# Where the modulation of a group of k-tiles stands in VectorE's queue, in a float32 decoder layer on one core

## The chip, the cores and the metric

The kernel runs on one core of a Trainium2 chip. The metric is device time in microseconds, from one launch; 1799.18 us is the median of three runs of the kernel before (1798.88 to 1799.37).

## The reference, cut to what matters

One layer of a decoder trunk: 256 tokens, model width 2048, everything in float32. The part that the change touches is the first:

```
mod = silu(c) @ w_ada + b_ada            # (2048) @ (2048, 6*2048): shift, scale, gate, twice
h   = rmsnorm(x, g_mix) * (1 + sc1) + sh1
z   = h @ w_in                           # (256, 2048) @ (2048, 16392)
```

The columns of `z` feed three causal token mixers (an mLSTM, a differential attention, a stick-breaking attention) and three gates; their outputs are projected, summed under the gates, projected again and added to `x`. A gated MLP with a causal convolution follows, with shift, scale and gate of its own. The result is the residual stream, 256 by 2048.

## The kernel before, in words

Every large product is made of three passes over TensorE. A weight slab is cut into a high half, which ScalarE rounds (`A.copy`, L330), and a low half, the rest, which VectorE subtracts (L332). The activations are held as two halves too, `hi` and `lo` of `h`. High times high, low activations times high weights, and high activations times low weights are summed in PSUM. A slab has four k-tiles of 128 rows (or two, in the first visits) by 512 (or 440) columns; it is one transfer into a raw buffer (`weights`, L319 to L336), and the raw buffer comes free when the low half has been made. There are three raw buffers for slabs of four k-tiles, and the same three carry the modulation's weights; slabs of two k-tiles use another three. High and low halves have four buffers of two k-tiles each.

The modulation is a product of one row with a large matrix. It isn't made on TensorE: `ada_mac` multiplies each piece of `w_ada` by its column of silu(c) and adds it up on VectorE (L213 for the first piece of a group, L215 for the others). When the pieces of a group are done, TensorE sums over the partitions (`ada_sums`, L231), VectorE adds the biases and multiplies by g_mix (`b1` at L234, `a1` at L235 and L236), and `make_h` makes the group's `h` from the normalised and transposed x: ScalarE scales and shifts into a scratch tile (L439), rounds that to the high half, and VectorE subtracts to the low half (both in `split`, L393 and L394). The groups are k-tiles 0-1, 2-3, 4-7, 8-11 and 12-15.

Since h of later k-tiles is not there at the start, the first thirteen column blocks of `w_in` are made in visits: `visit` takes some blocks from the k-tile that they have reached to a later one, and `partial` adds what the visit brings to the sum kept in SBUF (L512, on VectorE), or leaves it in PSUM for the first two blocks (`kept`). The visits take blocks 0 to 8 to k-tile 2, blocks 9 to 12 to 4, blocks 0 to 8 to 4, blocks 0 to 9 to 8, blocks 10 to 12 to 12 and blocks 0 to 6 to 12; then every block is finished. So h of k-tiles 4-7 is first used by the slabs of blocks 0 and 1, 48 matmuls each. Between the slabs, `tick` draws pieces of the modulation out of a generator at a set rate, so that program order interleaves slabs, sums and pieces.

What runs when is settled when the kernel is built. A planner goes through the program with costs of its own and puts on each engine's queue what is ready by its reckoning, earlier instructions of the program first. On the chip each of VectorE's instructions then runs in that order, and waits for its inputs. `tc.issue_after(ins)` adds an edge for the planner alone: what is traced inside the block goes behind `ins` on the queue of that engine. The kernel before has such edges for the first visits (`hold`) and for the late modulation.

Of the kernel before, what the change touches and what calls it, by code (L numbers as in the profile page):

```python
# [13 lines left out]
ALU = mybir.AluOpType  # L14
# [4 lines left out]
S = 256  # L19
# [20 lines left out]
def kernel(  # L40
# [32 lines left out]
    def sidewide(name):  # L73
        return tmp.tile([P, 512], F32, tag="sidewide", name=name, bufs=4)

    def small(name):
        return tmp.tile([P, 256], F32, tag="small", name=name, bufs=3)

    V, A, T = nc.vector, nc.scalar, nc.tensor
# [44 lines left out]
    gmix_c = colsA[:, 0:16]  # L124
# [56 lines left out]

    side = deque()
    ada = deque()
    state = {"ada": 0.0, "side": 0.0, "split": None, "load": None, "hold": None, "h": 0, "started": False}

    def pump(queue, n):
        done = 0
# [12 lines left out]
    def tick():  # L200
        for key, queue in (("ada", ada), ("side", side)):
# [2 lines left out]
            state[key] -= n  # L204
            pump(queue, n)


    def ada_mac(accs, raw, kt0, nk):
        for k in range(nk):
            kt = kt0 + k  # L210
            acc = accs[kt % len(accs)]
            if kt < len(accs):
                V.tensor_scalar(acc, raw[:, k, :], ccol[:, kt:kt + 1], None, ALU.mult)  # L213
            else:
                state["mac"] = V.scalar_tensor_tensor(acc, raw[:, k, :], ccol[:, kt:kt + 1], acc, ALU.mult, ALU.add)  # L215

# [9 lines left out]
    def ada_sums(accs, k0, nk):  # L226

        pm = adaps.tile([P, 512], F32, tag="adaps", name="pm")
        for i, acc in enumerate(accs):
            for k in range(2 * nk):  # L230
                T.matmul(pm[:, k:k + 1], lhsT=acc[:, k * P:(k + 1) * P], rhs=ones[:, 0:1],  # L231
                         start=k + i == 0, stop=i == len(accs) - 1, skip_group_check=True)
        ks = slice(k0, k0 + nk)
        V.tensor_tensor(b1[:, ks], pm[:, 0:nk], bsh1_c[:, ks], ALU.add)  # L234
        V.tensor_tensor(a1[:, ks], pm[:, nk:2 * nk], bsc1_c[:, ks], ALU.add)  # L235
        V.tensor_tensor(a1[:, ks], a1[:, ks], gmix_c[:, ks], ALU.mult)  # L236
        make_h(k0, k0 + nk)

    def ada_first(k0):
# [78 lines left out]
    def weights(rows, nk, n, hold=None):  # L318
        if nk == 2:  # L319
            raw = adap.tile([P, 2, 512], F32, tag="ada", name="raw2")  # L320
        else:
            raw = rawp.tile([P, 4, 512], F32, tag="raw", name="raw")
        with tc.issue_after(state["load"].ins) if not state["started"] else nullcontext():
            state["started"] = True
            state["load"] = nc.sync.dma_start(raw[:, :nk, :n], rows.rearrange("(k p) f -> p k f", p=P))
        his, los = [], []
        for k0 in range(0, nk, 2):
            hi = hip.tile([P, 2, 512], F32R, tag="hi", name="hi")
            lo = lop.tile([P, 2, 512], F32R, tag="lo", name="lo")
            A.copy(hi[:, :, :n], raw[:, k0:k0 + 2, :n])  # L330
            with tc.issue_after(hold.ins) if hold else nullcontext():
                state["split"] = V.tensor_tensor(lo[:, :, :n], raw[:, k0:k0 + 2, :n], hi[:, :, :n].bitcast(F32),  # L332
                                                 ALU.subtract)
            his.append(hi)
            los.append(lo)
        return his, los  # L336
# [54 lines left out]
    def split(hi, lo, src):  # L391

        A.copy(hi, src)  # L393
        return V.tensor_tensor(lo, src, hi.bitcast(F32), ALU.subtract)  # L394
# [31 lines left out]
            A.copy(xnT[k2 // 4][:, (k2 % 4) * 512:(k2 % 4 + 1) * 512], pb)  # L426

    def make_h(kt0, kt1):
        ts = []
        for kt in range(kt0, kt1):  # L430
            t = small("ht")
            ts.append(t)
            hi, lo = hact[0](kt), hact[1](kt)
            if kt0 == 0:
                A.activation(hi, xnT_k(kt), AF.Identity, scale=a1[:, kt:kt + 1], bias=b1[:, kt:kt + 1])
                V.tensor_scalar(t, xnT_k(kt), a1[:, kt:kt + 1], b1[:, kt:kt + 1], ALU.mult, ALU.add)
                state["split"] = V.tensor_tensor(lo, t, hi.bitcast(F32), ALU.subtract)
            else:
                A.activation(t, xnT_k(kt), AF.Identity, scale=a1[:, kt:kt + 1], bias=b1[:, kt:kt + 1])  # L439
                state["split"] = split(hi, lo, t)  # L440
        if kt0 == 0:
            state["first"] = state["split"]
        state["h"] = kt1
# [44 lines left out]
    def shaped(src, dst):  # L488
        return src.rearrange("p (a b) -> p a b", a=dst.shape[1]) if len(dst.shape) == 3 else src

    def partial(ci, kt0, kt1):
# [12 lines left out]
        for b in range(2):  # L504
            for cs, d in dest(b):
                if ci in kept:
                    if kt1 == KD:
                        A.activation(d, shaped(acc[b][:, cs], d), AF.Copy, scale=scale)
                elif kt0 == 0:
                    A.activation(d, shaped(acc[b][:, cs], d), AF.Copy, scale=scale)  # L510
                else:
                    V.scalar_tensor_tensor(d, shaped(acc[b][:, cs], d), scale, d, ALU.mult, ALU.add)  # L512
        tick()

    kept = {}
# [325 lines left out]
            tick()  # L841


    rates["ada"] = 0.0
    def ada_rest():
        yield from ada_columns(3, bsh2_c, b2)
# [213 lines left out]
```

## Time and profile before

| what | value |
|---|---|
| median of three runs | 1799.18 us (1798.88 to 1799.37) |
| the profiled execution: its own time | 1798.04 us |
| the profiled execution: span from the first to the last instruction | 1796.1 us |
| TensorE matmuls busy | 1759.3 us, 98% of the span |
| VectorE busy | 1327.8 us, 74% |
| ScalarE busy | 909.8 us, 51% |
| mean granted TensorE clock | 0.993 |
| moved by DMA | 423.31 MB, 236 GB/s |

Busy time is the union of an engine's instructions; the rest of the span it stood idle. The profiled execution's own time is 1.9 us above its span. PE is TensorE, PEld its weight loads, DVE VectorE, ACT ScalarE, SPq the queue of SyncE, which issues the transfers of weights. L332 is line 332 of the kernel before. A row of a stretch has its start and end, its length, the busy time (and number of instructions) of PE, PEld, DVE, ACT and POOL, the granted clock as a share of 2.4 GHz, the share of time that the 16 DMA engines were busy, and GB/s. A row of the order in time has start and duration in us, engine, line, operation, names, shapes and, in brackets, how long the engine had been idle and what ended that.

### The profile page before, as it was taken

The numbers are of one execution on the slowest core, as the hardware profiler recorded it, in microseconds if no ns is written. First come the engines' busy times: TensorE is split into PE (matmuls) and PEld (weight loads), VectorE is DVE, ScalarE is ACT, GpSimd is POOL, SyncE is SP. The second block draws the span as 40 slices with busy tenths as digits, with TensorE's granted clock in tenths as the row PEclk, the third lists the DMA queues.
The fourth block names the chain that finished last, engine by engine and source line by source line (L and its number), as shares of the span: only waits on it lengthen the run. The fifth ranks groups of instructions, "written<-read, shape, count | busy, mean of one in ns | idle before, by whom it ended". The sixth has DMA issues, their size and how long they took to land.

```text
span 1796.1 us, 23640 instructions
## 1 busy us (share of the span) xinstructions
PE 1759.3 (98%) x9101; PEld 1506.9 (84%) x9101; DVE 1327.8 (74%) x1781; ACT 909.8 (51%) x1234; POOL 16.4 (1%) x44
## 2 busy tenths in 40 slices
PE   6989999999999999999999999999999999999998
PEld 5888999888878887888888878888888888888887
DVE  6899766888988788777896577888875556666654
ACT  6533345666565556544444455555553345555432
POOL 2000000000000000000000000000000000000000
PEclk8999999999999999999999999999999999999999
DMA  9989855776777567578896547777755555555563
GB/s 337 354 279 314 300 181 187 242 248 235 248 256 256 199 237 252 200 260 285 311 317 238 183 157 257 249 258 267 269 200 190 199 195 189 189 188 188 187 212 116
DMA packets 219728, 423.31 MB, mean 236 GB/s; under 512 B 9026, under 2 KB 31674, under 8 KB 219104
## 3 DMA queue, kind: packets, MB, share of 16 engines
q1 hardware_dynamic: 217328, 417.44, 68.8%
q0 software_dynamic: 1008, 2.23, 0.4%
q10 hardware_dynamic: 1280, 2.14, 0.3%
q8 instruction: 71, 1.16, 0.3%
q14 instruction: 41, 0.34, 0.1%
HBM read 419.68 MB, written 2.10 MB: 235 GB/s over the span
## 4 chain that ended last, share of the span: by engine, by line
PE 94%; DVE 2%; DMA 2%; ACT 1%; issue 0%; SPq 0%; ACTq 0%; DVEq 0%
PE gp L375 52%; PE acch L361 32%; PE kept L377 3%; PE gp L377 2%; DMA raw<-in_w_in_dram 1%; DVE lo L332 1%; DVE quads L215 1%; DMA raw<-in_w_ada_dram 1%; PE psc L640 0%; ACT hi L330 0%; PE pm L231 0%; SPq L251 0%; PE psc L765 0%; DVE acc L215 0%; PE pr L309 0%
## 5 line engine op out<-in xcount | busy, mean ns | idle before, releaser
L332 DVE TENSOR_TENSOR lo<-raw,hi 128x1024 fp32r<-128x1024 f32 (+1 forms) x608 | 729.1, 1208 | 352.2 <-ACT hi L330 323.0
L330 ACT CAST hi<-raw 128x1024 fp32r<-128x1024 f32 (+1 forms) x608 | 622.4, 1040 | 684.3 <-PE gp L375 361.7
L361 PE MATMUL acch<-h,hi 128*128 128x512 f32 x1664 | 504.9, 396 | 1.8 <-DVE h L976 1.8
L375 PE MATMUL gp<-hi,h 128*128 128x512 f32 (+1 forms) x1600 | 408.0, 385 | 5.9 <-ACT hi L330 5.3
L361 PEld LDWEIGHTS acch<-h,lo 128*128 128x128 f32 x1664 | 297.4, 189 | 62.4
L375 PEld LDWEIGHTS gp<-hi,h 128*128 128x128 f32 x1600 | 296.8, 188 | 58.4 <-ACT hi L330 7.0
L361 PE MATMUL acch<-h,lo 128*128 128x256 f32 x1664 | 310.2, 279 | 0.0
L361 PEld LDWEIGHTS acch<-h,hi 128*128 128x128 f32 x1664 | 264.7, 189 | 14.1 <-DVE h L976 2.1
L375 PE MATMUL gp<-lo,h 128*128 128x512 f32 (+1 forms) x800 | 227.2, 383 | 0.0
L215 DVE SCALAR_TENSOR_TENSOR acc<-araw,ccol,acc 128x512 f32<-128x512 f32 x240 | 179.0, 746 | 5.1 <-DMA araw<-in_w_ada_dram 3.6
L375 PEld LDWEIGHTS gp<-lo,h 128*128 128x128 f32 x800 | 149.6, 188 | 25.6 <-issue 0.7
L375 PE MATMUL gp<-hi,ath 128*128 128x512 f32 x352 | 136.9, 389 | 0.0
L375 PE MATMUL gp<-hi,atl 128*128 128x512 f32 x352 | 136.9, 389 | 0.0
L375 PE MATMUL gp<-lo,ath 128*128 128x512 f32 x352 | 105.7, 389 | 0.0
L375 PEld LDWEIGHTS gp<-hi,ath 128*128 128x128 f32 x352 | 66.1, 188 | 13.7
L375 PEld LDWEIGHTS gp<-lo,ath 128*128 128x128 f32 x352 | 66.1, 188 | 13.7
L375 PEld LDWEIGHTS gp<-hi,atl 128*128 128x128 f32 x352 | 66.1, 188 | 13.7
L215 DVE SCALAR_TENSOR_TENSOR quads<-raw,ccol,quads 128x1024 f32<-128x1024 f32 x45 | 57.6, 1280 | 1.9 <-DMA raw<-in_w_ada_dram 1.4
L375 PE MATMUL gp<-hi,mgl 128*128 128x512 f32 x128 | 50.3, 393 | 0.0
L375 PE MATMUL gp<-hi,mgh 128*128 128x512 f32 x128 | 50.1, 392 | 0.0
L377 PE MATMUL kept<-h,hi 128*128 128x256 f32 x256 | 42.3, 306 | 4.3 <-DVE h L394 1.9
L1000 DVE SCALAR_TENSOR_TENSOR y<-gsum,cols,y 128x255 f32<-128x255 f32 (+1 forms) x88 | 41.1, 478 | 3.7 <-ACT y L998 3.5
(353 smaller groups left out, 1558.6 us busy)
## 6 DMA issues: line engine op xcount, KB each, us to landing
raw<-in_w_in_dram SPq DMA_DIRECT2D x98, 1024.0 KB, 5.1
raw<-in_w_up_dram SPq DMA_DIRECT2D x88, 1024.0 KB, 5.1
araw<-in_w_ada_dram SPq DMA_DIRECT2D x128, 512.0 KB, 5.7
raw<-in_w_down_dram SPq DMA_DIRECT2D x44, 1024.0 KB, 5.1
raw<-in_w_ada_dram SPq DMA_DIRECT2D x62, 512.0 KB, 5.6
raw<-in_w_branch_dram SPq DMA_DIRECT2D x24, 1024.0 KB, 5.2
raw<-in_w_in_dram SPq DMA_DIRECT2D x25, 880.0 KB, 4.8
raw<-in_w_out_dram SPq DMA_DIRECT2D x16, 1024.0 KB, 5.1
```

Of the source, the lines that this page charges most:

```text
L215: state["mac"] = V.scalar_tensor_tensor(acc, raw[:, k, :], ccol[:, kt:kt + 1], acc, ALU.mult, ALU.add)
L330: A.copy(hi[:, :, :n], raw[:, k0:k0 + 2, :n])
L332: state["split"] = V.tensor_tensor(lo[:, :, :n], raw[:, k0:k0 + 2, :n], hi[:, :, :n].bitcast(F32), ALU.subtract)
L361: T.matmul(acc[t][:, 0:m], lhsT=w[k // 2][:, k % 2, sl], rhs=ah(s0 + k)[:, 0:m], start=start, stop=s0 + k == kt1 - 1 and w is wl, skip_gro ...
L375: T.matmul(o, lhsT=a(s0 + k)[:, sl], rhs=wk[:, :n], **kw)
L377: T.matmul(o, lhsT=wk[:, sl], rhs=a(s0 + k), **kw)
L1000: V.scalar_tensor_tensor(yf[:, sft:S], src[:, 0:S - sft], wc(2 - sft), yf[:, sft:S], ALU.mult, ALU.add)
```

## The change

Three kinds of edges are added and one scratch pool is changed.

- `state["chain"]` remembers the last instruction that makes `a1` (L236). The low halves of weight slabs (when no `hold` is given) and the adds of partial sums that are traced after it go behind it on VectorE's queue. After the visits it is set to nothing.
- `state["low"]` remembers the last low half of h of a group. The first piece of each later group of the modulation goes behind it.
- In `make_h` the scratch tile `ht` comes from the pool `sidewide`, which has four buffers of 512 columns, of which it uses 256; before it came from `small`, which has three. The list `ts`, which nothing read, is gone.

```diff
--- before.py
+++ after.py
@@ -181,7 +181,7 @@
 
     side = deque()
     ada = deque()
-    state = {"ada": 0.0, "side": 0.0, "split": None, "load": None, "hold": None, "h": 0, "started": False}
+    state = {"chain": None, "low": None, "ada": 0.0, "side": 0.0, "split": None, "load": None, "hold": None, "h": 0, "started": False}
 
     def pump(queue, n):
         done = 0
@@ -204,13 +204,17 @@
             state[key] -= n
             pump(queue, n)
 
+    def behind(key):
+        return tc.issue_after(state[key].ins) if state[key] else nullcontext()
+
 
     def ada_mac(accs, raw, kt0, nk):
         for k in range(nk):
             kt = kt0 + k
             acc = accs[kt % len(accs)]
             if kt < len(accs):
-                V.tensor_scalar(acc, raw[:, k, :], ccol[:, kt:kt + 1], None, ALU.mult)
+                with behind("low"):
+                    V.tensor_scalar(acc, raw[:, k, :], ccol[:, kt:kt + 1], None, ALU.mult)
             else:
                 state["mac"] = V.scalar_tensor_tensor(acc, raw[:, k, :], ccol[:, kt:kt + 1], acc, ALU.mult, ALU.add)
 
@@ -233,7 +237,7 @@
         ks = slice(k0, k0 + nk)
         V.tensor_tensor(b1[:, ks], pm[:, 0:nk], bsh1_c[:, ks], ALU.add)
         V.tensor_tensor(a1[:, ks], pm[:, nk:2 * nk], bsc1_c[:, ks], ALU.add)
-        V.tensor_tensor(a1[:, ks], a1[:, ks], gmix_c[:, ks], ALU.mult)
+        state["chain"] = V.tensor_tensor(a1[:, ks], a1[:, ks], gmix_c[:, ks], ALU.mult)
         make_h(k0, k0 + nk)
 
     def ada_first(k0):
@@ -328,7 +332,7 @@
             hi = hip.tile([P, 2, 512], F32R, tag="hi", name="hi")
             lo = lop.tile([P, 2, 512], F32R, tag="lo", name="lo")
             A.copy(hi[:, :, :n], raw[:, k0:k0 + 2, :n])
-            with tc.issue_after(hold.ins) if hold else nullcontext():
+            with tc.issue_after(hold.ins) if hold else behind("chain"):
                 state["split"] = V.tensor_tensor(lo[:, :, :n], raw[:, k0:k0 + 2, :n], hi[:, :, :n].bitcast(F32),
                                                  ALU.subtract)
             his.append(hi)
@@ -426,10 +430,8 @@
             A.copy(xnT[k2 // 4][:, (k2 % 4) * 512:(k2 % 4 + 1) * 512], pb)
 
     def make_h(kt0, kt1):
-        ts = []
         for kt in range(kt0, kt1):
-            t = small("ht")
-            ts.append(t)
+            t = sidewide("ht")[:, 0:S]
             hi, lo = hact[0](kt), hact[1](kt)
             if kt0 == 0:
                 A.activation(hi, xnT_k(kt), AF.Identity, scale=a1[:, kt:kt + 1], bias=b1[:, kt:kt + 1])
@@ -437,7 +439,7 @@
                 state["split"] = V.tensor_tensor(lo, t, hi.bitcast(F32), ALU.subtract)
             else:
                 A.activation(t, xnT_k(kt), AF.Identity, scale=a1[:, kt:kt + 1], bias=b1[:, kt:kt + 1])
-                state["split"] = split(hi, lo, t)
+                state["low"] = state["split"] = split(hi, lo, t)
         if kt0 == 0:
             state["first"] = state["split"]
         state["h"] = kt1
@@ -509,7 +511,8 @@
                 elif kt0 == 0:
                     A.activation(d, shaped(acc[b][:, cs], d), AF.Copy, scale=scale)
                 else:
-                    V.scalar_tensor_tensor(d, shaped(acc[b][:, cs], d), scale, d, ALU.mult, ALU.add)
+                    with behind("chain"):
+                        V.scalar_tensor_tensor(d, shaped(acc[b][:, cs], d), scale, d, ALU.mult, ALU.add)
         tick()
 
     kept = {}
@@ -841,6 +844,7 @@
             tick()
 
 
+    state["chain"] = None
     rates["ada"] = 0.0
     def ada_rest():
         yield from ada_columns(3, bsh2_c, b2)
```

## Rows read from the trace of the kernel before

**Rows 1.** Stretches of the span, with busy time, granted clock and transfers.

```profile
30.00:210.00 180.00, 169.01 (x991) 155.33 (x991) 157.97 (x195) 76.94 (x111) 0.00 (x0) 0.97 0.93 320
...
210.00:1000.00 790.00, 790.00 (x3932) 666.35 (x3932) 620.69 (x889) 428.05 (x590) 4.59 (x10) 1.00 0.72 244
...
96.00:114.00 18.00, 15.21 (x80) 12.60 (x78) 18.00 (x34) 7.46 (x14) 0.00 (x0) 0.94 0.66 221
...
108.00:114.00 6.00, 3.85 (x18) 2.94 (x16) 6.00 (x13) 1.17 (x3) 0.00 (x0) 0.81 0.68 229
...
114.00:120.00 6.00, 5.06 (x29) 5.07 (x30) 5.96 (x6) 1.83 (x2) 0.00 (x0) 0.63 0.92 322
...
150.00:198.00 48.00, 46.16 (x237) 42.50 (x236) 43.58 (x60) 19.13 (x26) 0.00 (x0) 1.00 0.94 317
```

**Rows 2.** Order in time, 44 to 64 us: start, us, engine, line, operation [idle before].

```profile
48.17 0.74 DVE L213 TENSOR_SCALAR quads<-raw,ccol 128x1024 f32<-128x1024 f32 x1
...
48.94 1.28 DVE L215 SCALAR_TENSOR_TENSOR quads<-raw,ccol,quads 128x1024 f32<-128x1024 f32 x1
...
50.25 6.29 SPq L325 DMA_DIRECT2D raw<-in_w_in_dram  x3
...
52.64 0.76 DVE L394 TENSOR_TENSOR h<-ht,h 128x256 fp32r<-128x256 f32 x2 [0.20 <-ACT h L393]
...
55.07 3.05 DVE L332 TENSOR_TENSOR lo<-raw,hi 128x880 fp32r<-128x880 f32 x3 [1.66 <-ACT hi L330]
...
62.40 1.76 PE L375 MATMUL gp<-hi,h 128*128 128x440 f32 x8
```

**Rows 3.** Weight transfers issued by L325 from 36 to 60 us.

```profile
DMA to landing us min/median/max: 5.0/8.0/9.9
```

**Rows 4.** Order in time, 94 to 117 us.

```profile
95.85 0.75 DVE L213 TENSOR_SCALAR quads<-raw,ccol 128x1024 f32<-128x1024 f32 x1
...
96.36 1.84 PE L231 MATMUL pm<-ones,quads 128*128 128x1 f32 x16
...
101.48 0.15 DVE L234 TENSOR_TENSOR b<-pm,colsA 128x4 f32<-128x4 f32 x1
...
104.98 0.15 DVE L236 TENSOR_TENSOR a<-a,colsA 128x4 f32<-128x4 f32 x1
...
105.17 1.58 ACT L439 ACTIVATE ht<-xnT,b,a 128x256 f32<-128x256 f32 x3 [0.26 <-DVE a L236]
...
107.42 1.22 DVE L332 TENSOR_TENSOR lo<-raw,hi 128x1024 fp32r<-128x1024 f32 x1
...
110.75 0.74 PE L377 MATMUL kept<-h,hi 128*128 128x256 f32 x4 [1.71 <-DVE h L394]
...
113.65 0.42 DVE L394 TENSOR_TENSOR h<-ht,h 128x256 fp32r<-128x256 f32 x1
...
114.94 2.29 PE L377 MATMUL kept<-h,hi 128*128 128x256 f32 x9 [1.19 <-ACT hi L330]
```

**Rows 5.** The chain that ended last: start, us, what.

```profile
108.67 5.10 DMA raw<-in_w_in_dram
...
114.94 11.65 PE kept L377 x82
```

**Rows 6.** Order in time, 148 to 180 us.

```profile
150.45 1.84 PE L231 MATMUL pm<-ones,quads 128*128 128x1 f32 x16
...
154.29 0.75 DVE L213 TENSOR_SCALAR quads<-raw,ccol 128x1024 f32<-128x1024 f32 x1
...
163.43 0.42 DVE L394 TENSOR_TENSOR h<-ht,h 128x256 fp32r<-128x256 f32 x1
...
177.41 2.87 PE L375 MATMUL gp<-hi,h 128*128 128x440 f32 x13 [1.40 <-ACT hi L330]
```

**Rows 7.** Order in time, 205 to 224 us.

```profile
215.64 2.36 DVE L332 TENSOR_TENSOR lo<-raw,hi 128x1024 fp32r<-128x1024 f32 x2 [2.64 <-ACT hi L330]
...
221.08 0.28 PE L231 MATMUL pm<-ones,quads 128*128 128x1 f32 x2
```

## The prediction, made before the changed kernel was run

> **What bounds the kernel now.** I read the profile from coarse to fine. First, stretches of the whole span: from 210 to 1000 us TensorE is busy 790.00 of 790.00 us at clock 1.00, so nothing upstream can make that part shorter. From 30 to 210 us, the stretch in which the modulation is still being summed and where every edit of the diff acts, it is busy 169.01 of 180 us: 11.0 us of holes, and a mean granted clock of 0.97 [rows 1]. Those holes and the clock are all that the change can win; all that it can lose is a longer hole there. Next, narrower stretches: at 108 to 114 us TensorE is busy 3.85 of 6 us at 0.81, and at 114 to 120 us at 0.63; at 96 to 114 us VectorE is busy 18.00 of 18.00 us while the transfers run at a share of 0.66 [rows 1]. So there the bound is VectorE's queue: it frees the raw buffers, and a raw buffer that comes free late lets its next transfer start late. At 150 to 198 us the transfers are at 0.94 and VectorE has some idle time, 43.58 of 48 us busy [rows 1]. Last, the order of instructions in time: it shows how the four groups of modulation (k-tiles 2-3, 4-7, 8-11, 12-15) pass through VectorE's queue, and what TensorE waits for.
>
> **The change, group by group.** The number of instructions is the same before and after, and so is the shape of each; only their order on VectorE, and with it the time at which buffers come free, can differ. So every term is a wait that goes or comes.
>
> *k-tiles 2-3.* The h of this group is already split at 52.64 with 0.20 us idle ahead of it, so nothing stood in its way [rows 2]. What moves is the first two pieces of the next group (48.17 and 48.94, 0.74 and 1.28 us, together 2.0): they must now follow the last h, which ends at 53.40 (52.64 + 0.76). VectorE is idle for 1.66 us right there, up to 55.07 [rows 2]. Two microseconds into a hole of 1.66 leaves 0.35 for the three splits behind it. The buffer of those two pieces is the second effect: SyncE issues a weight transfer at 50.25, just as the second piece ends (48.94 + 1.28 = 50.22) [rows 2]; it would be free at 53.40 + 2.0 = 55.4, so the transfer starts 5.2 us later. Transfers of this line took 5.0 at least and 8.0 in the median in this stretch [rows 3]. Its high halves then take about 1 us on ScalarE, and I place its first matmuls at 62.40 [rows 2]. So it is ready at 55.4 + 5.0 + 1 = 61.4 (no loss) or 55.4 + 8.0 + 1 = 64.4 (2.0 lost). With fewer transfers in flight, it should be nearer to the 5.0. I take +0.3 and keep 0 to +2.0.
>
> *k-tiles 4-7, the one that matters.* The column sums run on TensorE from 96.36 to 98.20. The shift (b) comes at 101.48 and the finished scale (a) at 104.98, so 6.8 us after the sums there is still no scale; ScalarE then makes three pieces of h (0.53 us each, 1.58 for three), has no fourth buffer, and the last low half runs from 113.65 to 114.07 [rows 4]. TensorE stands 1.71 us for a low half of h at 110.75, and 1.19 us at 114.94, there for the high half of the next slab's weights [rows 4]. After the change b and a follow the sums at about 98.3 to 98.6; four pieces of 0.53 and their high halves take ScalarE to about 102, and the low halves are done near 103. So h comes some 11 us earlier, and that wait is gone.
>
> What is late next is a weight transfer. The chain goes from the split at 107.42 (1.22, ends 108.64) to the transfer at 108.67 (5.10), through ScalarE's high half, to TensorE at 114.94 [rows 4, 5]. VectorE had no idle time from 96 to 114 us [rows 1], so that split ends later by everything that is now put ahead of it: four low halves of h (0.42 each, 1.7) and the hole while the queue stands for the column sums. The first piece of the next group, which filled 95.85 to 96.6 [rows 4], may no longer do so; adds of partial sums that were traced earlier can, and of the rest I count 0.5 idle. So the split ends 2.2 later and the second slab's weights are ready at 114.94 + 2.2 = 117.1.
>
> Yet TensorE has less left to do by then. At 114.94 it had 82 matmuls of the first two slabs of k-tiles 4-7 ahead of it, 11.65 us up to 126.59 [rows 5]; a slab is 48, so 34 of the first slab were undone, because h was late. With h there by 103 the first slab runs as soon as the earlier visits are out, about 109, and at the same 11.65 / 82 = 0.142 us takes 6.8, to 115.8. At 117.1 only 48 are left, again 6.8 us: 123.9 in place of 126.6. That is the gain, -2.7. The best end would be that all holes of 96 to 120 us go (18.00 - 15.21 = 2.8 and 6 - 5.06 = 0.9) and the clock stays up (0.19 x 6 + 0.37 x 6 = 3.4) [rows 1]: -7.1. The worst is that TensorE's order still puts the second slab's matmuls ahead of what is left of the first, as at 114.94: then the 2.2 are simply added.
>
> The clock in these rows fell to 0.81 and 0.63, between its levels of 1.2 and 2.4 GHz, around a run of holes, the longest 1.71 us [rows 1, 4]. The Trainium skill, TensorE: Matmul & The Clock Gate, section Why this matters for your kernels, warns of idle gaps between bursts of matmuls, since the array goes back to half rate after them. [...]
>
> *k-tiles 8-11.* Sums end at 152.29 and the last low half of h is at 163.43, but TensorE shows no wait for h here; its hole is at 177.41, 1.40 us, for a high half of weights [rows 6]. So there is nothing to win, and a cover is lost: the piece at 154.29 (0.75) and the one after it (1.28 by the row at 48.94) filled the time in which ScalarE makes h, and now come after. The hole is 0 to 2.0 us on a VectorE that has 4.4 us of idle time in 48 [rows 1]; what passes to TensorE comes through the raw buffers, as a longer wait at 177.41. I take +0.5 and keep 0 to +2.0.
>
> *k-tiles 12-15.* The last two column-sum matmuls run only at 221.08, while two weight splits that were traced after them run at 215.64 (2.36 for two) [rows 7]. They must now wait for 221.6. TensorE turns to these weights at about 221.2, and two thirds of its matmuls take the high half alone, so I cost this at nothing; without that cover it is 221.6 + 2.4 - 222.2 = +1.8, and the cover fails if TensorE's order wants a low half after the first eight matmuls.
>
> The fourth buffer only takes away the wait of the fourth piece, which is inside the 4-7 term.
>
> Sum: +0.3 - 2.7 + 0.5 + 0 = -1.9. The profiled execution took 1798.04 (span 1796.1 and 1.9 around it), which gives 1796.1; it lies 1.1 under the median of 1799.18, and against that the forecast is 1797.3. A change of this kernel is told from none at about 0.2%, 3.6 us, so this is no change that can be told.
>
> **Rivals.**
> 1. *The holes close altogether.* For it: VectorE is the bound at 96 to 114 with the transfers at 0.66 [rows 1], so a planner that sees h early may put the splits ahead of the next pieces of modulation; then the second slab isn't late and the clock has no reason to fall. Against it: the sum of VectorE's work ahead of that split grows. Price: -7.1 + 0.3 + 0.5 = -6.3, 1792.9.
> 2. *The gain is given back.* h is late for TensorE in one group of four, and from 150 to 198 the transfers are at 0.94 [rows 1]; what TensorE gains at 126 it then stands out at holes like the one at 177.41. Price: -2.7 + 2.7 + 0.3 = +0.3, 1799.5. This is also the case in which the change does nothing, since three of the four groups had their h in time.
> 3. *The queue's head blocks (slower).* One mechanism: b and a stand in VectorE's queue while TensorE has not reached the column sums; splits and pieces behind them hold the raw buffers, and weight transfers start late. The place is the split that ended at 108.64. It decides from the point at which the second slab ends later than 126.6: its weights would have to be ready after 126.6 - 6.8 = 119.8, that is 4.9 later than now, a split that ends after 113.5. Below this TensorE has work, above it each microsecond counts. Price with the upper ends: 2.2 + 2.0 + 1.4 (the 177.41 wait doubled) = +5.6, 1804.8. For it: no idle time in that queue; against it: the sums were done 3.3 us before b ran, so the head would not stand long.
>
> The Trainium skill, PSUM - Partial Sum Buffer, section Engine vs sequencer instructions, says that VectorE's queue is strictly first in, first out. By it rival 3 has no way round a blocked head; the rows agree in that b and a, ready at 98.20, ran only when the queue reached them at 101.48 and 104.98 [rows 4].
>
> **How the numbers follow.** Forecast 0.34, within 1795 to 1798.6 for itself; rival 1 0.29; rival 2 0.17; rival 3 0.20. Faster by over 0.2%: rival 1 and the lower edge of the forecast, 0.34. Slower by over 0.2%: most of rival 3, 0.18. Within: 0.48. The range leaves out about a tenth on each side: the end of rival 1 below 1792 and the end of rival 3 above 1803.5.
>
> **What would show it.** Right: b and a within 1 us of the column sums in all groups; no wait of TensorE for h after 105; the transfer of 108.67 starting at 110 to 112; TensorE done with the second slab at about 124, and the wait near 177 no shorter against the matmul count. Rival 1: clock 1.00 from 108 to 120. Rival 3: that split ending after 113.5, or TensorE's holes from 48 to 72 growing by over 1 us. The forecast is wrong if the holes of 30 to 210 us change by more than 3.6 us in either direction, or if new holes come after 210.

## The result, and the profile after

The change made the kernel slower: 1806.28 us in the median of six runs (1803.74 to 1807.08) against 1798.20 in six runs of the kernel before beside them (1795.05 to 1799.37), ratio 1.0041 with a 95% interval of 1.0030 to 1.0052. The prediction, 1797.3 in a range of 1792.0 to 1803.5, was wrong. The profiled execution took 1803.74 us (span 1802.0; before 1796.1).

Stretches of the kernel after, in the columns of [rows 1]:

```profile
30.00:210.00 180.00, 163.80 (x924) 149.14 (x924) 150.23 (x186) 73.71 (x108) 0.00 (x0) 0.96 0.89 308
210.00:1000.00 790.00, 789.21 (x3956) 666.84 (x3956) 623.83 (x893) 426.65 (x590) 4.59 (x10) 1.00 0.72 244
96.00:114.00 18.00, 17.37 (x88) 14.97 (x87) 15.92 (x31) 8.15 (x14) 0.00 (x0) 0.81 0.52 181
108.00:114.00 6.00, 6.00 (x33) 5.71 (x33) 6.00 (x11) 0.00 (x0) 0.00 (x0) 0.79 0.51 168
114.00:120.00 6.00, 3.52 (x30) 3.32 (x28) 5.15 (x5) 0.89 (x1) 0.00 (x0) 1.00 0.82 278
150.00:198.00 48.00, 42.09 (x207) 38.24 (x206) 40.23 (x55) 16.61 (x24) 0.00 (x0) 0.96 0.84 286
```

The first row holds the loss: from 30 to 210 us TensorE is busy 5.2 us less (163.80 against 169.01), VectorE 7.7 less, and the transfers run at 308 GB/s in place of 320. That is 12 x 180 us = 2.16 MB less, 6.8 us at the old rate. From 96 to 114 TensorE is busier than before (17.37 us and 88 matmuls against 15.21 and 80, at a granted clock of 0.81 against 0.94), but the transfers fell from a share of 0.66 to 0.52, and that comes out at 114 to 120 (3.52 against 5.06). The large loss is the last row: 42.09 against 46.16, transfers 0.84 against 0.94. From 210 to 1000 us only 0.8 us is lost (789.21 of 790).

What TensorE waited for from 36 to 230 us, before and then after (total, times, longest):

```profile
PE gp L375 <- ACT hi L330: 5.3, 5, 1.6
PE kept L377 <- DVE h L394: 1.9, 2, 1.7
PE kept L377 <- ACT hi L330: 1.2, 1, 1.2
```

```profile
PE gp L379 <- ACT hi L334: 11.4, 8, 3.2
PE kept L381 <- ACT hi L334: 3.2, 2, 2.7
```

The wait for h is gone, as the change meant. Waits for high halves of weights, which ScalarE makes once a slab has landed, went from 6.5 to 14.6 us.

The order in time after, around the sums of k-tiles 4-7 (beside [rows 4]):

```profile
99.75 1.84 PE L235 MATMUL pm<-ones,quads 128*128 128x1 f32 x16
101.63 0.16 DVE L238 TENSOR_TENSOR b<-pm,colsA 128x4 f32<-128x4 f32 x1 [2.05 <-PE pm L235]
101.89 0.16 DVE L240 TENSOR_TENSOR a<-a,colsA 128x4 f32<-128x4 f32 x1
101.97 3.04 DVE L336 TENSOR_TENSOR lo<-raw,hi 128x880 fp32r<-128x880 f32 x3
...
109.81 0.88 SPq L271 DMA_DIRECT2D raw<-in_w_ada_dram  x2
...
110.22 0.75 DVE L398 TENSOR_TENSOR h<-ht,h 128x256 fp32r<-128x256 f32 x2
110.89 0.75 DVE L217 TENSOR_SCALAR quads<-raw,ccol 128x1024 f32<-128x1024 f32 x1
...
114.03 0.37 SPq L329 DMA_DIRECT2D raw<-in_w_in_dram  x1
...
120.21 2.03 PE L381 MATMUL kept<-h,hi 128*128 128x256 f32 x10 [2.69 <-ACT hi L334]
```

The bias and scale follow the sums at once, and VectorE stands 2.05 us for them with three splits behind. The buffer that comes free at 109.8 goes to the modulation; the second slab's transfer goes at 114.03 (before: 108.67 [rows 5]), when two pieces of k-tiles 8-11 have been used, and TensorE stands 2.69 us for it.

Around the sums of k-tiles 8-11 (beside [rows 6]):

```profile
156.32 0.17 DVE L240 TENSOR_TENSOR a<-a,colsA 128x4 f32<-128x4 f32 x1
...
163.59 0.42 DVE L398 TENSOR_TENSOR h<-ht,h 128x256 fp32r<-128x256 f32 x1
163.70 0.37 SPq L329 DMA_DIRECT2D raw<-in_w_in_dram  x1
163.92 0.75 DVE L217 TENSOR_SCALAR quads<-raw,ccol 128x1024 f32<-128x1024 f32 x1
...
169.34 3.47 PE L379 MATMUL gp<-hi,h 128*128 128x440 f32 x16 [2.51 <-ACT hi L334]
...
171.62 0.37 SPq L329 DMA_DIRECT2D raw<-in_w_in_dram  x1
...
177.58 2.26 PE L379 MATMUL gp<-hi,h 128*128 128x440 f32 x8 [3.17 <-ACT hi L334]
```

The first piece of k-tiles 12-15, at 154.29 before, runs at 163.92. Waits of 2.51 and 3.17 us follow where there were waits of 0.44 (170.94) and 1.40.

To see where time is lost, I use the adds of `partial` (L512 before, L515 after) as marks: 86 of them, in the same order in every kernel. The table has the start of the 25th, 36th, 39th and 54th (149.4, 167.7, 182.1 and 238.9 us before) as a difference to the kernel before, from one profiled execution each:

| kernel | 25th | 36th | 39th | 54th | GB/s, 30 to 210 us |
|---|---|---|---|---|---|
| before | 0 | 0 | 0 | 0 | 320 |
| after | +0.3 | -0.5 | +7.0 | +8.3 | 308 |
| no_low | -3.4 | -3.2 | -1.3 | -0.1 | 321 |
| low_only | +0.2 | -0.2 | +7.1 | +5.5 | 311 |
| low_k4 | -1.2 | +2.4 | +1.8 | +1.2 | 318 |
| low_k8 | -2.0 | -1.8 | -1.7 | -0.9 | 323 |
| low_k12 | -0.5 | -0.9 | +5.4 | +3.3 | 315 |
| after_k8 | -0.4 | -0.6 | -0.4 | +0.3 | 320 |
| after_k12 | -3.8 | -3.9 | +3.1 | +2.6 | 317 |
| after_k48 | +1.0 | +2.4 | +6.2 | +7.3 | 309 |
| after_k812 | +0.6 | -1.6 | +5.4 | +3.4 | 315 |
| own12_before | -0.7 | -0.9 | +2.9 | +2.1 | 319 |
| own12_k12 | -0.4 | -0.9 | +3.9 | +2.3 | 318 |
| own12_after | +1.6 | +2.3 | +6.6 | +5.2 | 312 |
| spare_low | +3.8 | +3.5 | +4.0 | +6.3 | 310 |
| own812_after | +7.1 | +8.3 | +10.6 | +10.7 | 301 |

After is level with before up to 168 us, loses 7.5 us up to 182 and 1.3 more up to 239. Every kernel with the edge of k-tiles 12-15 and its pieces in raw buffers steps up by 6.2 to 7.5 us between the 36th and the 39th add; the others by 4.8 at most, and own12_before, which has no edge, by 3.8, so not all of the step is the edge's. A mark also holds what the granted clock of its one execution cost: before has 0.81 and 0.63 from 108 to 120 us [rows 1], no_low 1.00. The last two columns tell one thing twice: (320 - GB/s) x 180 / 320 is within 1.6 us of the 54th add's delay in all twenty kernels profiled. So work and transfers fall behind together; which comes first, the column can't say, and the experiments must.

### The profile page after: what moved, and what is told of

It is laid out like the page before. It is cut to its first block, busy times and chain, and to the rows that moved or that the text cites. A ratio compares the mean times of both kernels' runs of the same rounds, so it can differ in the third digit from the quotient of the medians.

```text
span 1802.0 us, 23638 instructions
## 1 busy us (share of the span) xinstructions
PE 1758.6 (98%) x9101; PEld 1505.7 (84%) x9101; DVE 1328.2 (74%) x1781; ACT 908.9 (50%) x1234; POOL 16.4 (1%) x44
## 4 chain that ended last, share of the span: by engine, by line
PE 92%; DVE 1%; DMA 1%; ACT 0%; issue 0%; ACTq 0%; DVEq 0%
PE gp L379 52%; PE acch L365 32%; PE gp L381 2%; PE kept L381 2%; DMA raw<-in_w_in_dram 1%; DVE lo L336 1%; PE psc L643 0%; ACT hi L334 0%; PE pm L235 0%; PE psc L768 0%; PE pr L313 0%; PE px L963 0%; PE pdt L628 0%; PE pmg L839 0%; PE ptf L701 0%
## 5 line engine op out<-in xcount | busy, mean ns | idle before, releaser
L334 ACT CAST hi<-raw 128x1024 fp32r<-128x1024 f32 (+1 forms) x608 | 622.4, 1040 | 695.7 <-PE gp L379 367.0
```

## Experiments

Each kernel was timed in five rounds beside the kernel before; a ratio is to that, over all rounds, with its 95% interval; it can differ by up to 0.0007 from the quotient of two medians. I start with the parts of the change.

**One kind of edge at a time.** `no_low` is the change without the edge on first pieces, `low_only` that edge alone, `chain_only` the edges behind the scale alone, `bufs_only` the four buffers alone.

```diff
# the edge on first pieces: no_low is the change without it, low_only has it alone
             if kt < len(accs):
-                V.tensor_scalar(acc, raw[:, k, :], ccol[:, kt:kt + 1], None, ALU.mult)
+                with behind("low"):
+                    V.tensor_scalar(acc, raw[:, k, :], ccol[:, kt:kt + 1], None, ALU.mult)
```

> The changed kernel without the edge that puts the first piece of a group behind the last low half of h; the edges behind the scale and the four buffers stay. Theory H (held buffers): the pieces that wait for h keep two of the three raw buffers full, so the weight transfer of the second slab of k-tiles 4-7 starts at 114.0 in place of 108.7, the transfers fall to a share of 0.24 at 102 to 108 us, and the same comes back near 163 us. Without this edge the two buffers come free again: time within 2 us of before or better (1795 to 1800), share at 102 to 108 us 0.5 or more, that transfer at 107 to 111. Theory Q (head of the queue): splits and adds stand behind a scale that waits for TensorE's column sums; then it stays slow, 5 to 8 us over before. Theory R (any new order of the plan costs): 3 to 8 us over before, and so for each of these four kernels.

> The kernel before with only the edge of the first piece behind the last low half of h. Theory H: it carries the loss, 5 to 9 us over before (1803 to 1807), with TensorE holes near 115 and near 167 to 177 as in the changed kernel. Theory Q: 0 to 2 us over before. Theory R: 3 to 8 us over.

> The kernel before with only the edges behind the scale (weight splits and adds of partial sums). Theory H: within 2 us of before; the forecast's gain of some 2 to 3 us at k-tiles 4-7 may show. Theory Q: 5 to 8 us over before. Theory R: 3 to 8 us over.

> The kernel before with only the fourth scratch buffer for unsplit h. All but theory R: within 1.5 us of before, since the 3.06 us that ScalarE stood for the fourth piece held up one low half of h by 1 to 2 us in one group. Theory R: 3 to 8 us over.

| kernel | median us | ratio |
|---|---|---|
| no_low | 1795.41 | 0.9992 (0.9982 to 1.0002) |
| low_only | 1803.69 | 1.0038 (1.0026 to 1.0050) |
| chain_only | 1797.32 | 1.0003 (0.9992 to 1.0014) |
| bufs_only | 1797.43 | 1.0004 (0.9996 to 1.0013) |

The edge on first pieces alone makes the loss; without it the change can't be told from before. Theories Q (the other edges) and R (any new order costs) fall, since chain_only and bufs_only are within 0.0004 of before. `no_low` is faster than the changed kernel, and is not shown to be faster than the kernel before. With h early and no piece held, its marks are 3.4 us ahead at 149 us, and the lead is used up by 239.

**One group's edge at a time.** The same edge only for the first piece of k-tiles 4-7, 8-11 or 12-15, by the number of k-tiles whose h has been made.

```diff
-                V.tensor_scalar(acc, raw[:, k, :], ccol[:, kt:kt + 1], None, ALU.mult)
+                with behind("low") if state["h"] == 12 else nullcontext():   # 8 in low_k8, 4 in low_k4
+                    V.tensor_scalar(acc, raw[:, k, :], ccol[:, kt:kt + 1], None, ALU.mult)
```

> The kernel before with the edge behind the last low half of h for one group alone, the first piece of k-tiles 8-11. Theory H (pieces that wait for h hold raw buffers): two of the three raw buffers are full from about 99 us until h of k-tiles 4-7 is split, the freed third carries more pieces, and the transfer of the second weight slab starts near 113; 2.5 to 5 us over before, a hole of TensorE of 2.5 to 3.5 us near 116, and nothing new near 167 to 177. Theory D (VectorE loses the time in which it may not work ahead, and the pieces then run in a burst ahead of splits): the loss goes with VectorE's idle time, which is 1.3 us in this group in the run with the edge alone: 1 to 2 us over before.

> The kernel before with that edge for the first piece of k-tiles 12-15 alone. Theory H: as above near 160 to 177, where TensorE's holes grow from 1.8 to 4 or more; 2.5 to 5 us over before, and nothing new near 116. Theory D: 0.5 to 2 us over before. In sum of this run and the one for 8-11: theory H 6 to 8 (the whole edge measured 6.8), with at most 1.5 left for the group 4-7.

> The kernel before with one edge alone: the first piece of k-tiles 4-7 behind the last low half of the h of k-tiles 2-3. The three edges of this kind together cost 6.8 us (1.0038), the one of k-tiles 8-11 alone 0.1 (1.0001), the one of k-tiles 12-15 alone 3.2 (1.0018). If the costs add up, what is left for this one is 3.5 us, 1.0019. Theory A (the transfer that waits for the buffer of the first two pieces goes at 55.3 in place of 50.25, its high halves then stand on ScalarE behind a copy of the slab before): holes of TensorE of about 1 us at 63.5 and at 76.2, the 25th add of partial sums (149.4 us in the kernel before) 1.5 to 2.5 us later, and the time 1.5 to 3.5 us longer. Rival: what is lost before 150 us is made up in the stretch from 150 to 210 us, where TensorE waits for transfers in any case: no change, 0.9994 to 1.0005.

Measured: low_k8 1.0001 (0.9992 to 1.0009), low_k12 1.0018 (1.0009 to 1.0027), low_k4 0.9998 (0.9988 to 1.0009). Only the last group's edge costs by itself: 3.2 us, as theory H expected (2.5 to 5). For k-tiles 8-11 both theories missed (2.5 to 5 and 1 to 2 us expected, 0.1 measured), and so did theory H's sum of the two (6 to 8 expected, 3.3 measured). Of theory A for k-tiles 4-7 the holes came (1.04 us at 63.35 and at 76.11) and the loss did not: the 25th add is 1.2 us ahead, not behind, and the rival's range holds the ratio.

SyncE's issues from 148 to 172 us show what the edge of k-tiles 12-15 does (L267 and L271: modulation, two transfers for two pieces; L325 and L329: a slab of weights). Kernel before:

```profile
148.55 0.88 SPq L267 DMA_DIRECT2D raw<-in_w_ada_dram  x2
151.72 0.37 SPq L325 DMA_DIRECT2D raw<-in_w_in_dram  x1
154.40 0.88 SPq L267 DMA_DIRECT2D raw<-in_w_ada_dram  x2
156.39 0.37 SPq L325 DMA_DIRECT2D raw<-in_w_in_dram  x1
...
165.07 0.37 SPq L325 DMA_DIRECT2D raw<-in_w_in_dram  x1
...
171.13 2.86 SPq L325 DMA_DIRECT2D raw<-in_w_in_dram  x2
```

low_k12, with the first piece that the edge holds and TensorE's wait:

```profile
148.04 0.88 SPq L271 DMA_DIRECT2D raw<-in_w_ada_dram  x2
151.21 0.37 SPq L329 DMA_DIRECT2D raw<-in_w_in_dram  x1
153.48 0.88 SPq L271 DMA_DIRECT2D raw<-in_w_ada_dram  x2
160.85 0.37 SPq L329 DMA_DIRECT2D raw<-in_w_in_dram  x1
161.94 0.75 DVE L217 TENSOR_SCALAR quads<-raw,ccol 128x1024 f32<-128x1024 f32 x1
...
169.51 0.37 SPq L329 DMA_DIRECT2D raw<-in_w_in_dram  x1
...
175.12 2.42 PE L379 MATMUL gp<-hi,h 128*128 128x440 f32 x8 [3.53 <-ACT hi L334]
```

Before, the first two pieces (154.29 [rows 6], then one more) give their buffer back and a slab goes at 156.39. With the edge, the pieces issued at 148.04 and 153.48 hold two of the three raw buffers until 164.0 and 169.5; the slab of 160.85 goes through the third, and the one of 169.51 into the buffer that the second pair of pieces gives back. In the 24 us before 172 three slabs start in place of four.

**The same edge, with the pieces elsewhere.** If held buffers are the cause, the edge must cost nothing when its pieces lie in other tiles. A first form of the test puts four pieces of k-tiles 8-11 and of 12-15 into the three 4 KB modulation buffers, in the kernel before (`spare_before`) and with all three edges (`spare_low`).

```diff
+            if k0 >= 8 and q < 2:
+                for k in range(2):
+                    half = adap.tile([P, 2, 512], F32, tag="ada", name="rawh")
+                    ...
+                    ada_mac([acc], half.rearrange("p i f -> p (i f)").unsqueeze(1), 2 * q + k, 1)
+                    yield
+                continue
             raw = rawp.tile([P, 2, 1024], F32, tag="raw", name="raw4")
```

> The kernel before, with the first four pieces of the groups 8-11 and 12-15 in the buffers of the two-k-tile slabs (4 KB a piece, three of them, idle by then but for three slabs) in place of the raw buffers; no new edge. It is the base of the next run. Theory H: the raw buffers carry more weights, 0 to 4 us under before. Theory D: within 1.5 us of before.

> That kernel with the edge of the first pieces behind h, all three groups. The pieces wait as long as before, in a place that no weight slab needs. Theory H: the loss is gone, within 2.5 us of the kernel with the pieces in those buffers and no edge (what is left is the group 4-7, whose pieces keep their place), no hole of over 2 us near 116 or 170. Theory D: VectorE may work ahead as little as with the edge alone, so 4 to 8 us over the kernel without the edge.

Measured: 1.0006 (0.9996 to 1.0015) and 1.0037 (1.0025 to 1.0050). By its expectation this was a miss for the theory of held buffers. By the marks it was not a clean test: the step between the 36th and 39th add shrank from 7.3 us (low_only) to 0.5, but 3.8 us were lost ahead of the 25th. The slabs of two k-tiles still use those three buffers then: the first two pieces of k-tiles 8-11 hold two of them until 108.71 and 110.03, and TensorE stands 3.15 us at 106.65 and 3.07 us at 114.12 for high halves of slabs.

The second form gives the fourth piece a free half of a work tile, and does so for k-tiles 12-15 alone: `own12_before` without an edge, `own12_k12` with the edge of low_k12.

```diff
+            if k0 == 12 and q < 2:
+                for k in range(2):
+                    own = (adap.tile([P, 2, 512], F32, tag="ada", name="own") if 2 * q + k < 3 else
+                           state["rows2"][:, 1024:2048].rearrange("p (i f) -> p i f", i=2))
+                    ...
```

> The control of the next run: the kernel before, with the first four pieces of k-tiles 12-15 in tiles of their own (three of the small modulation buffers and a free half of a work tile) and not in raw buffers; no edge. Both theories: no loss, 0.9980 to 1.0005, since the weights get two raw buffers more for a while and nothing else moves; under the theory of held buffers there may be a gain of up to 2 us, because the pieces hold a buffer for some time in the kernel before too.

> The edge of k-tiles 12-15 alone (1.0018 when the pieces were in raw buffers), with the first four pieces in tiles of their own. Theory H (held buffers): from 153 to 169 us two of the three raw buffers held pieces that had landed and waited for the low halves of h, and slabs of weights went through the third. With pieces elsewhere the loss goes: within 0.0005 of the control own12_before, transfers' share from 150 to 180 us 0.88 or more (0.78 with the edge and raw buffers), the 39th add of partial sums (182.1 in the kernel before, 187.5 with the edge) not over 2 us later than in the control. Rival Q (VectorE's own time: the pieces no longer fill its waits and come late, wherever they lie): 1.0013 to 1.0022 over the control, share near 0.78, the 39th add 4 us or more late.

Measured: own12_before 0.9999 (0.9990 to 1.0009), own12_k12 0.9997 (0.9989 to 1.0006); low_k12 had 1.0018 (1.0009 to 1.0027), and the intervals don't meet. The edge is the same and VectorE's pieces are as late (162.16 against 161.94); only the buffers differ, and the loss is gone. The theory of held buffers holds for this edge, and rival Q falls. The 39th add is 0.9 us behind the control's, as expected; the transfers' share from 150 to 180 us is 0.84, between low_k12's 0.78 and the 0.88 that was expected and that the control has. Slabs of own12_k12 in that stretch, and TensorE's longest wait:

```profile
149.09 0.38 SPq L342 DMA_DIRECT2D raw<-in_w_in_dram  x1
...
152.61 0.38 SPq L342 DMA_DIRECT2D raw<-in_w_in_dram  x1
...
161.08 0.37 SPq L342 DMA_DIRECT2D raw<-in_w_in_dram  x1
...
172.17 3.40 SPq L342 DMA_DIRECT2D raw<-in_w_in_dram  x2
...
177.79 3.67 PE L392 MATMUL gp<-hi,h 128*128 128x440 f32 x9 [2.90 <-ACT hi L347]
```

Three before 172 and the fourth at 172.17, with the first two early; low_k12 also has three before 172, and its fourth goes at 173.93. So the profiles alone show the cure faintly: at the 39th add the two kernels are 1.5 us apart (+5.4 and +3.9). Part of that is the clock. The nine matmuls behind the wait at 177.79 took 3.67 us, where thirteen took 2.87 at full rate [rows 6], at a mean granted clock of 0.95 from 150 to 180 us: 3.67 - 9 x 2.87 / 13 = 1.7 us of the +3.9. In low_k12 the eight at 175.12 lose 0.7 us in this way. The verdict rests on the timed runs, eleven and twelve of them, and the clock doesn't explain it: among the runs whose mean granted clock is 0.995 or more, the median of low_k12 is 2.9 us above that of the kernel before beside it (5 runs against 18), that of own12_k12 0.6 us below (7 against 24).

**The edges inside the whole change.** `after_k8`, `after_k12`, `after_k48` and `after_k812` are the whole change with the edge on those groups' first pieces only; `own12_after` is the whole change with the tiles of own12_k12.

```diff
-                with behind("low"):
+                with behind("low") if state["h"] == 8 else nullcontext():   # == 12; < 12; >= 8
```

> The whole change without the edges of k-tiles 4-7 and of k-tiles 12-15: the edge of k-tiles 8-11, the edges behind the scale, and the four buffers stay. If effects add up: 0.9992 (without any such edge) and 0.0001 for this one, 0.9993, 1795 to 1797 us. Rival: with h of k-tiles 4-7 early the second slab is waited for, and the edge makes it later, as in the whole change: 1.0008 or more.

> The whole change without one edge, that of the first piece of k-tiles 12-15. Theory H1 (the loss is made by this edge alone, by the raw buffers that it holds): the loss goes, ratio 0.9992 to 1.0010, transfers' share of 150 to 180 us 0.88 or more (0.79 in the whole change), the 39th add of partial sums (182.1 in the kernel before, 189.1 in the whole change) within 2 us of the kernel before. Theory H2 (the three edges add to one another: each single one was at or near nothing, so part of the 6.8 us of all three is made only where the work of k-tiles 4-7 and 8-11 is late already): 1.0015 to 1.0025, since about half of the loss stays without this edge.

> The whole change with only one edge of the three on first pieces, that of k-tiles 12-15. The four buffers and the edges behind the scale make the adds at 150 us come 3.4 us earlier when no piece is held. Theory H1: this edge has the whole loss of the change, 1.0030 to 1.0045. Theory H2: it has its own part only, 1.0010 to 1.0025.

> The whole change, with the first four pieces of k-tiles 12-15 in tiles of their own (as in own12_k12, where this took the whole loss of the edge away). Theory H1: ratio 0.9992 to 1.0012, and the 39th add within 3 us of own12_before's 185.0. Theory H2: the buffers cure only the part of that edge, 1.0015 to 1.0025. Rival Q (VectorE's own time): no cure, 1.0030 to 1.0045.

> The whole change without one edge, that of the first piece of k-tiles 4-7. The whole change was 1.0041, without its edge of 12-15 1.0018, with that of 8-11 alone 1.0005, with that of 12-15 alone 0.9999, with none 0.9992. Theory B (each edge has its own share, added to one another): 0.9992 + 0.0013 + 0.0007 to 0.0023, so 1.0012 to 1.0028. Rival D (the edge of k-tiles 4-7 is needed, because it puts the second stretch of pieces behind): no loss without it, 0.9992 to 1.0006.

| edges on first pieces, with the rest of the change | ratio |
|---|---|
| none (no_low) | 0.9992 (0.9982 to 1.0002) |
| 8-11 (after_k8) | 1.0005 (0.9996 to 1.0014) |
| 12-15 (after_k12) | 0.9999 (0.9990 to 1.0008) |
| 4-7 and 8-11 (after_k48) | 1.0018 (1.0009 to 1.0027) |
| 8-11 and 12-15 (after_k812) | 1.0023 (1.0014 to 1.0031) |
| all (after) | 1.0041 (1.0030 to 1.0052) |
| all, tiles of their own for 12-15 (own12_after) | 1.0013 (1.0004 to 1.0022) |

H1 falls: without the last edge there is still 1.0018, and with it alone 0.9999. H2 has after_k48 right and after_k12 wrong (1.0010 to 1.0025 expected); own12_after and after_k8 lie between the ranges of their two theories. From a row to the next with one edge more the ratio rises by 0.0007 to 0.0024 (1.3 to 4.3 us, each with an uncertainty of about 0.0013), and it takes all three to make 1.0041 out of 0.9992. For after_k812 B's range holds and D falls. That the costs are plain sums is not shown: in the kernel before, the three edges one at a time come to 0.0017 in sum and all three together to 0.0038. Tiles of their own for one group take 0.0028 off, over half of the loss.

**Tiles of their own for two groups.** As own12_after and own12_before, for k-tiles 8-11 too (`k0 >= 8`).

> The whole change, with the first four pieces of k-tiles 8-11 and of k-tiles 12-15 in tiles of their own. With those of 12-15 alone the ratio went from 1.0041 to 1.0013. Theory B (each edge costs what its held raw buffers keep from being transferred: by 210 us the whole change had moved 308 GB/s x 180 us against 320, 2.2 MB or 6.8 us less): the held buffers of 8-11 go too, what is left is the edge of k-tiles 4-7, 0.9992 to 1.0008, transfers from 30 to 210 us at 316 GB/s or more. Rival C (what is left of the loss is made on TensorE and VectorE by the later h and pieces, not by buffers): 1.0010 to 1.0020, below 313 GB/s.

> The control: the kernel before with the same tiles of their own and no edge. Both theories: 0.9985 to 1.0005, as own12_before (0.9999); if it is slower than 1.0010, the tiles do harm by themselves and own812_after has to be read against it.

Measured: own812_after 1.0051 (1.0038 to 1.0065), own812_before 1.0006 (0.9997 to 1.0015). Both theories missed: it got worse. Its order at 107 to 117 us:

```profile
107.59 0.75 DVE L222 TENSOR_SCALAR quads<-own,ccol 128x1024 f32<-128x1024 f32 x1
108.28 1.08 DVE L353 TENSOR_TENSOR lo<-raw,hi 128x880 fp32r<-128x880 f32 x1
108.36 0.82 SPq L280 DMA_DIRECT2D own<-in_w_ada_dram  x2
109.38 0.38 SPq L346 DMA_DIRECT2D raw<-in_w_in_dram  x1
...
116.25 3.30 PE L396 MATMUL gp<-hi,h 128*128 128x440 f32 x8 [3.64 <-ACT hi L351]
```

As in spare_low, slabs of two k-tiles still use the small buffers at that time. The piece that the edge holds runs at 107.59 and only then gives its buffer to the next piece's transfer (108.36); another piece holds the second buffer until 110.55. So these slabs go one after another through the third: the one of 109.38 follows the split that ends at 109.36, and TensorE then stands 3.64 us. The edge's wait came back through another buffer, earlier; without an edge (own812_before) the 25th add is 1.8 us ahead of the kernel before, not 7.1 behind. How much of the costs of the edges of k-tiles 4-7 and 8-11 is held buffers is therefore not settled: it was not tried in tiles that nothing else uses.

No version beats both kernels: no_low, the best, is 0.9992 with 1 inside its interval.

## Why the prediction was wrong

The step that failed is the price of the edges on first pieces. The prediction counted what a moved piece costs VectorE, +0.3, a part of 2.2 and +0.5 us, and asked only in one group when its buffer comes back. By the runs these three edges cost 0.0049 together (1.0041 against 0.9992), 8.8 us; the edges behind the scale and the four buffers, without them, come to -1.4, which can't be told from nothing. The first piece of a group follows the h of the group before, so the edge of k-tiles 4-7 stands in the prediction's paragraph on k-tiles 2-3, and so on.

**K-tiles 2-3** (+0.3, bounds 0 and +2.0): the delayed transfer was forecast, the reason for its cost was wrong. Rows of the kernel after:

```profile
55.30 1.35 SPq L329 DMA_DIRECT2D raw<-in_w_in_dram  x2
...
62.08 0.54 ACT L512 ACTIVATE dk<-gp 128x440 f32<-128x440 f32 x1 [3.71 <-PE gp L379]
62.51 1.74 ACT L334 CAST hi<-raw 128x880 fp32r<-128x880 f32 x2
```

The transfer goes at 55.30, forecast 55.4. Its high halves come at 62.51 because they stand in ScalarE's queue behind a copy that waits 3.71 us for TensorE, where I had counted 1 us of ScalarE's work and no queue; TensorE's matmuls of this slab start at 63.48 in place of 62.40 [rows 2]. Alone this edge is 0.9998, within the bounds; within the whole change it comes to 0.0018, 3.2 us (1.0041 against after_k812), more than the upper bound, though the uncertainty reaches below it.

**K-tiles 4-7** (-2.7): without the edges of the first pieces (no_low) the 25th add is 3.4 us ahead; in the whole change it is 0.3 behind. The lead is of the size that was forecast, but that is luck, as rows of no_low show:

```profile
108.00:114.00 6.00, 5.12 (x33) 4.59 (x32) 6.00 (x11) 2.00 (x2) 0.00 (x0) 1.00 0.59 191
114.00:120.00 6.00, 6.00 (x53) 6.00 (x52) 5.96 (x8) 0.00 (x0) 0.00 (x0) 1.00 1.00 343
```

The clock is 1.00 where the kernel before had 0.81 and 0.63, which is 3.4 us by the prediction's own sum, and which the forecast had left to rival 1; TensorE's holes from 96 to 120 us shrink by 1.0 us alone (3.7 before, 2.7 here). The term had the second slab ready at 117.1; in the whole change it came at 120.21, past the 119.8 from which rival 3 decides. I had counted 0.5 us of idle VectorE (it was 2.05) and low halves done near 103 (the last two start at 110.22). And I followed the wrong holder: not the split of 107.42 [rows 4] frees the buffer for the second slab, but the second piece of k-tiles 8-11, which the edge holds until h is done. The Trainium skill, PSUM - Partial Sum Buffer, section Engine vs sequencer instructions, has VectorE's queue strictly first in, first out; the trace agrees, since three splits ran from 101.97, after the 2.05 us that b waited, though ScalarE had begun the high halves of two of them at 95.93 and 97.13.

**K-tiles 8-11** (+0.5, bounds 0 and +2.0): here the failure is plainest. "So there is nothing to win, and a cover is lost" priced the edge as VectorE's time and left the rest to "a longer wait at 177.41". Its edge, on the first piece of k-tiles 12-15, cost 3.2 us alone and 0.0023, 4.1 us, within the change (1.0041 against after_k48). By the marks the change loses 7.5 us between 168 and 182, of which 3.8 stay without this edge (after_k48). For k-tiles 2-3 I had asked when the held pieces give their buffer back. Here the same question has its answer in [rows 6]: pieces that ran at 154.29 now follow the h of 163.43, so their buffer comes back 9 us later, in a stretch where the transfers run at 0.94 [rows 1]. For this edge own12_k12 shows that it is the buffer and not VectorE; for the other two the cause of their share stays open.

**K-tiles 12-15** (0, up to +1.8): +1.3 from the 39th to the 54th add, within the bound.

**The rivals.** Rival 3 came nearest: raw buffers held behind the queue's head, at +5.6 and a chance of 0.20; the medians are 8.1 us apart. But its head was b and a, and the edges that make these a head cost nothing by themselves (chain_only 1.0003). The head that costs is the first piece, which waits for h, and the largest step of the marks is between 168 and 182 us, not at the split that ended at 108.64; that its price came near is partly luck. Rival 1 is out for the change: the clock from 108 to 114 was 0.79, and the holes did not close. Rival 2, gain given back, is what no_low does, the change without the edges on first pieces: 3.4 us ahead at 149, 0.1 at 239. The prediction's own sign of being wrong came true: TensorE's holes from 30 to 210 us grew from 11.0 to 16.2 us, by more than 3.6.

**The arithmetic of the range.** Terms of three groups had upper bounds of 2.0, 2.0 and 1.8, the last two set by VectorE's own time. The held buffer has no such bound: it lasts as long as h takes after the sums.

## What to carry to other kernels

Before an instruction is moved back in a queue, ask which buffer its inputs hold and which transfer waits for that buffer; where transfers run at nine tenths of the time, the hold can cost more than the instruction's microsecond: in low_k12 two buffers came back 7.6 and 4.4 us later (164.03 against 156.39, 169.51 against 165.07), and the edge cost 3.2 us. Landed data whose reader waits for a long chain should not sit in a pool that feeds the bound engine; moved to another pool that also feeds it, as in own812_after (1.0051), it cost no less. And edges that cost 0 to 0.18% one by one can cost 0.4% together, so the whole has to be timed beside its parts.

## What the hardware showed

From the 54th add to 1064 us the delay of after stays at 8.0 to 8.3 us; at the end it is 5.9. Of the difference 2.1 us come from one place, where the next product starts after a wait for h. Rows of before and of after, the stretch from 1040 to 1100 and the first matmuls:

```profile
1040.00:1100.00 60.00, 56.16 (x297) 48.03 (x296) 43.78 (x69) 34.52 (x57) 0.00 (x0) 0.94 0.53 183
1056.09 2.50 PE L361 MATMUL acch<-h,hi 128*128 128x512 f32 x5 [1.84 <-DVE h L976]
```

```profile
1040.00:1100.00 60.00, 56.16 (x300) 47.88 (x300) 43.53 (x67) 38.66 (x63) 0.00 (x0) 1.00 0.51 175
1064.05 1.43 PE L365 MATMUL acch<-h,hi 128*128 128x512 f32 x5 [1.84 <-DVE h L980]
```

The wait is 1.84 us in both, and in both a wait of 2.00 us and a dozen 128-column matmuls stand ahead of it. In before the last two of these already take 0.67 us for 0.49 in after, so the clock had fallen by then. In before the granted clock of the stretch is 0.94 and five matmuls take 2.50 us, in after 1.00 and 1.43: the lower of the two levels (1.2 and 2.4 GHz) for the first microseconds in one execution and not in the other, with the same code there. In seven of the twenty profiled executions, after among them, the span is 2.3 to 2.5 us less late than the 54th add, in the others 0 to 0.5; so a single profile of this kernel can mislead by over 2 us, and effects of that size need repeated timings.
